# Experts: one gather and one addition of 4 KB rows each, empty slots left out, matmuls held to program order

## The chip, the cores and the metric

The kernel runs on one core of a Trainium2 chip. The metric is the device time of one execution in microseconds (us). The engines of the core are TensorE (PE, with its weight load PEld), VectorE (DVE), ScalarE (ACT), GpSimd (POOL) and SyncE (SP); 16 DMA engines move data between HBM and SBUF. SP, ACT and POOL issue the DMAs.

## What is computed

The reference is a transformer block with a mixture of experts, followed by a second block (FFN, attention, state space, FFN, gated embedding). Only the experts of the first block matter here. Every one of 1024 tokens of 1024 features chooses two of 32 experts; an expert is a SwiGLU of width 256. Everything is float32.

```python
weights = g_p * e_p / jnp.sum(e_p, axis=-1, keepdims=True)      # two per token
expert = g_sel * EXPERTS_PER_GROUP + e_idx
...
def block_ffn(args):
    xb_i, e = args
    return (jax.nn.silu(xb_i @ w_gate[e]) * (xb_i @ w_up[e])) @ w_down[e]
...
out = jnp.zeros((T + 1, D), yb.dtype).at[buf_tok].add(yb * buf_w[:, None])
...
x = layer_norm(DEEPNORM_ALPHA * x + (1.0 + gt2) * y, ln2_g[l], ln2_b[l])
```

## The kernel before, in words

**Ahead of the experts.** `wo_last` (L1091) makes, for each of 8 groups of 128 tokens, the input of the experts (`h2`) and the residual already scaled (`x1`), and stores both in DRAM: `h2d` and `r1d`, each as two tensors of [1024, 512], one for each half of the features (L1088, L1111, L1114). The router (L1116 and the lines up to L1353) counts the tokens of each expert and builds, with 16 small matmuls, one column per expert with the tokens in its 104 slots (`CAP`). `slot_rows` (L1314) makes two tables of it: `table`, in which an empty slot names row 0, and `dest`, in which an empty slot names a row beyond 1023.

**One expert.** `gather` (L1355) fetches the rows of its slots with two indirect DMAs from GpSimd, one for each half of 512 features (2 KB a row), into tiles of the pool D. `expert_rows` (L1365) transposes them on TensorE, eight transposes, and splits the result into a high and a low part. `expert_up` (L1377) multiplies them with the gate and the up weights, 16 contraction steps of three matmuls (`mm3`: high x high, high x low, low x high), and forms silu(gate) x up, called the product here. `expert_turn` (L1389) transposes the product, two transposes, into `aT`. `expert_down` (L1398) multiplies it with the down weights, four matmuls of 512 columns, scales each half into a tile `y` of the small pool tmp, and adds it to `r1d` in DRAM with an indirect DMA that accumulates, one for each half; rows beyond 1023 are left out there. A tile may be written again only when those who read it are done, so `y`, the product `a` and other users of tmp wait for each other.

**Weights.** An expert has 3 x 1 MB of weights. `load_weights` (L1139) loads each matrix with four DMAs of 256 KB on SP's queue, in program order. Gate and up weights go to pool A (26 tiles), are split into high and low parts (`split_weights`, L1151; every fourth low part is made on GpSimd, the others on VectorE), and their parts lie in B and W. Down weights are used unsplit; `wide` (L1131) places them in turn in buffers of the pools raw, sub and tmpG.

**The loop** (L1414) runs over 32 experts. In turn e it gathers the rows of e + 2, splits the gate weights of e + 1, issues up of e, the row transposes of e + 1, down of e - 1 and the transposes of the product of e, splits the up weights of e + 1, and issues the loads of gate and up of e + 4 and of down of e + 2. A scheduler with a model of its own then sets the order on each engine; only what `keep_in_program_order` marks keeps its place among the marked. Here that is SP's weight loads; `pin` (L1363) is the identity, so the matmuls of the experts may move.

**Behind the loop** stands a second loop for experts with more than 104 tokens (L1444), which with these inputs runs no turn: the trace has 64 gathers, two for each expert. Then the first FFN begins with loads of `r1d`.

Of the kernel before, what the change touches and what calls it, by code (L numbers as in the profile page):

```python
# [32 lines left out]
T = 1024  # L33
# [184 lines left out]
def kernel(ctx: ExitStack, tc: tile.TileContext, I, C, out, taps=None, stop=99):  # L218
# [869 lines left out]
    h2d = [dr.tile([T, NH], F32, name=f"h2d{n}") for n in range(2)]  # L1088
    r1d = [dr.tile([T, NH], F32, name=f"r1d{n}") for n in range(2)]
    bl = bkB("bl")  # L1090
    def wo_last(t):  # L1091
# [14 lines left out]
        for n in range(2):  # L1106
            x = tD("x1")
            nc.scalar.activation(x, xr[:, half(n)], AF.Identity, bias=nm, scale=rs)
            nc.vector.tensor_mul(h2[n], x, sc2[n])
            nc.vector.tensor_add(h2[n], h2[n], sh2[n])  # L1110
            nc.sync.dma_start(h2d[n][t * 128:(t + 1) * 128, :], h2[n])  # L1111
            nc.gpsimd.tensor_mul(x, x, lg[n])
            nc.gpsimd.tensor_add(x, x, lb[n])
            nc.sync.dma_start(r1d[n][t * 128:(t + 1) * 128, :], x)  # L1114
            tap("x1", lambda a: a[t * 128:(t + 1) * 128, half(n)], x)
# [15 lines left out]
    def wide(n):  # L1131

        o = []
        for al in ((raw, raw), (raw, sub), (sub, None))[n]:
            t_ = al("wr") if al else None
            o += [t_[:, half(i)] if al else tmpG("wr") for i in range(2)]
        return o

    def load_weights(e, part, n=1, up=None):  # L1139
# [57 lines left out]
    def expert_loads(e, part=("gate", "up", "down")):  # L1197
        if e < 32:
            loaded[e] = loaded.get(e, []) + load_weights(e, part, e % 3)
# [14 lines left out]
    expert_loads(2)  # L1214
    expert_loads(3, ("gate", "up"))
    if stop <= 3:
        return

# [95 lines left out]
    def slot_rows(ps, n, src, dst):  # L1314
# [8 lines left out]
    table, dest, wslot = ctile("table", 32, I32), ctile("dest", 32, I32), const(32, "wslot")  # L1323
    tabled = slot_rows(bt[0:CAP, 0:32], 32, table, dest)
# [29 lines left out]

    def gather(rows):  # L1355

        xg = [tD("xg") for _ in range(2)]
        for n in range(2):
            nc.gpsimd.indirect_dma_start(out=xg[n][0:CAP, :], out_offset=None, in_=h2d[n],
                                         in_offset=bass.IndirectOffsetOnAxis(ap=rows[0:CAP, :], axis=0))  # L1360
        return xg

    pin = lambda i: i  # L1363

    def expert_rows(xg):  # L1365

        xT = []
        for h in range(2):
            b = bkB()
            for k in range(4):  # L1370
                nc.tensor.transpose(b[:, k * CAP:(k + 1) * CAP], xg[h][0:CAP, k * 128:(k + 1) * 128], ident[0:CAP, 0:CAP])
# [17 lines left out]
    def expert_turn(a_):  # L1389
        b = bkB()  # L1390
        for f in range(2):
            nc.tensor.transpose(b[:, f * CAP:(f + 1) * CAP], a_[:, f * 128:(f + 1) * 128], ident[0:CAP, 0:CAP])
        aT = tD("aT")[:, 0:2 * CAP]
# [14 lines left out]
    gathered[0] = gather(table[:, 0:1])  # L1408
    gathered[1] = gather(table[:, 1:2])
# [4 lines left out]
    for e in range(32):  # L1414
        if e < 30:
            gathered[e + 2] = gather(table[:, e + 2:e + 3])
# [27 lines left out]
    with tc.For_i(0, nc.values_load(nextra[0:1, 0:1], min_val=0, max_val=XMAX)) as ik:  # L1444
# [13 lines left out]
        xrows, xdest, xws = small(1, "xrows", I32), small(1, "xdest", I32), small(1, "xws")  # L1458
        slot_rows(bt[0:CAP, 0:1], 1, xrows, xdest)
# [7 lines left out]
        expert_down(expert_turn(expert_up(expert_rows(gather(xrows)), ws)), wd, xdest, xws)  # L1467
# [23 lines left out]
    def second_loads():  # L1491
        for t in range(8):
            for n in range(2):
                xr2[t, n] = tA("xr2")
                tc.keep_in_program_order(nc.sync.dma_start(xr2[t, n], r1d[n][t * 128:(t + 1) * 128, :]))
# [1218 lines left out]
```

## Time and profile before

| | us |
|---|---|
| median of 3 runs (3518.17 to 3523.24) | 3522.32 |
| the profiled execution | 3528.53 |
| its span, first to last instruction | 3526.7 |
| TensorE busy | 3286.4 (93%) |
| VectorE busy | 2444.1 (69%) |
| GpSimd busy | 1598.0 (45%) |
| ScalarE busy | 1484.4 (42%) |

A profile is one execution. Its times count from the start of the span; the experts run from 770 to 1175 us. TensorE's "granted clock" is the share of its full speed (2.4 GHz) that it was given. The "DMA share" is the mean busy share of the 16 DMA engines; it can exceed 1 a little, since transfers overlap. In the queue rows q1 is SP's queue and q0 GpSimd's.

### The profile page before, as it was taken

The numbers are of one execution on the slowest core, as the hardware profiler recorded it, in microseconds if no ns is written. First come the engines' busy times: TensorE is split into PE (matmuls) and PEld (weight loads), VectorE is DVE, ScalarE is ACT, GpSimd is POOL, SyncE is SP. The second block draws the span as 40 slices with busy tenths as digits, with TensorE's granted clock in tenths as the row PEclk, the third lists the DMA queues.
The fourth block names the chain that finished last, engine by engine and source line by source line (L and its number), as shares of the span: only waits on it lengthen the run. The fifth ranks groups of instructions, "written<-read, shape, count | busy, mean of one in ns | idle before, by whom it ended". The sixth has DMA issues, their size and how long they took to land. (4 is left out here: it accounts for less than half of the span.)

```text
span 3526.7 us, 49670 instructions
## 1 busy us (share of the span) xinstructions
PE 3286.4 (93%) x16788; PEld 2678.4 (76%) x16788; DVE 2444.1 (69%) x4146; ACT 1484.4 (42%) x2818; POOL 1598.0 (45%) x1228
## 2 busy tenths in 40 slices
PE   7998998979889789999999899999999999998998
PEld 5687887767666568887788777778778788886888
DVE  8857467777666676665976885577655866668685
ACT  5554434235554543232443233455623433324456
POOL 3533002357667467778511435522001587776011
PEclk9998999979999899999999999989999999999999
DMA  8421114579999523326643363543145223347433
GB/s 291 147 72 41 34 43 132 181 253 284 318 308 293 162 86 112 99 96 226 216 138 102 123 203 120 148 135 97 51 142 201 78 97 119 99 177 245 125 99 114
DMA packets 305650, 529.33 MB, mean 150 GB/s; under 512 B 67889, under 2 KB 82610, under 8 KB 305394
## 3 DMA queue, kind: packets, MB, share of 16 engines
q1 hardware_dynamic: 265328, 449.64, 39.4%
q10 hardware_dynamic: 25570, 53.91, 4.9%
q0 software_dynamic: 14496, 22.59, 2.8%
q8 instruction: 134, 2.20, 0.3%
q14 instruction: 122, 1.00, 0.1%
HBM read 409.55 MB, written 121.62 MB: 151 GB/s over the span
## 5 line engine op out<-in xcount | busy, mean ns | idle before, releaser
L284 PE MATMUL b<-x,wh 128*128 128x512 f32 x992 | 392.2, 396 | 3.9 <-ACT wh L277 3.9
L288 PE MATMUL b<-x,wl 128*128 128x512 f32 x992 | 390.4, 394 | 1.8 <-DVE wl L278 1.7
L287 PE MATMUL b<-x,wh 128*128 128x512 f32 x992 | 388.5, 392 | 0.0
L343 POOL TENSOR_TENSOR acc<-acc,sqt 128x512 f32<-128x512 f32 x42 | 62.7, 1492 | 519.1 <-ACT sqt L342 515.6
L278 DVE TENSOR_TENSOR wl<-S,wh 128x512 fp32r<-128x512 f32 x176 | 209.2, 1192 | 84.6 <-ACT wh L277 49.9
L284 PE MATMUL b<-ah,wh 128*128 128x512 f32 x560 | 221.0, 397 | 9.8 <-ACT wh L277 9.8
L288 PE MATMUL b<-ah,wl 128*128 128x512 f32 x560 | 213.9, 395 | 14.6 <-DVE wl L278 14.5
L288 PEld LDWEIGHTS b<-x,wl 128*128 128x128 f32 x992 | 186.7, 188 | 47.8 <-DVE wl L278 3.5
L287 PE MATMUL b<-al,wh 128*128 128x512 f32 x560 | 222.3, 397 | 0.0
L284 PEld LDWEIGHTS b<-x,wh 128*128 128x128 f32 x992 | 187.1, 189 | 45.2 <-ACT wh L277 4.9
L1158 DVE TENSOR_TENSOR wl<-wr,wh 128x512 fp32r<-128x512 f32 x186 | 168.4, 919 | 74.3 <-ACT wh L1157 69.6
L287 PEld LDWEIGHTS b<-x,wh 128*128 128x128 f32 x992 | 186.9, 188 | 42.7
L277 ACT CAST wh<-S 128x512 fp32r<-128x512 f32 x176 | 108.3, 618 | 242.5 <-PE b L287 203.2
L278 DVE TENSOR_TENSOR wl<-raw,wh 128x512 fp32r<-128x512 f32 (+1 forms) x187 | 144.7, 781 | 78.7 <-ACT wh L277 74.2
L1157 ACT CAST wh<-wr 128x512 fp32r<-128x512 f32 x256 | 157.0, 620 | 83.4 <-PE b L287 41.5
L277 ACT CAST wh<-raw 128x512 fp32r<-128x512 f32 (+1 forms) x187 | 112.2, 610 | 178.3 <-PE b L287 88.4
L288 PE MATMUL b<-hnh,wl 128*128 128x512 f32 (+1 forms) x480 | 178.4, 372 | 0.0
L284 PE MATMUL b<-hnh,wh 128*128 128x512 f32 (+1 forms) x480 | 178.3, 372 | 0.0
L287 PE MATMUL b<-hnl,wh 128*128 128x512 f32 (+1 forms) x480 | 177.1, 369 | 0.0
L1749 POOL TENSOR_TENSOR c<-c,rb 128x512 f32<-128x512 f32 x80 | 124.3, 1563 | 108.4 <-DVE c L1745 108.4
L284 PE MATMUL b<-wh,xTh 128*104 128x256 f32 x512 | 154.5, 302 | 4.2 <-ACT xTh L277 4.2
L284 PE MATMUL b<-xh,wh 128*128 128x512 f32 x384 | 151.4, 400 | 4.2 <-ACT xh L1528 2.4
(890 smaller groups left out, 9768.9 us busy)
## 6 DMA issues: line engine op xcount, KB each, us to landing
ffn_pair<-c SPq DMA_DIRECT2D x140, 256.0 KB
act<-ffn_pair SPq DMA_DIRECT2D x140, 256.0 KB
wr<-in_moe_w_gate SPq DMA_DIRECT2D x128, 256.0 KB
wr<-in_moe_w_up SPq DMA_DIRECT2D x128, 256.0 KB
wr<-in_moe_w_down SPq DMA_DIRECT2D x128, 256.0 KB
wm<-in_w_mod SPq DMA_DIRECT2D x96, 256.0 KB
wu<-in_ffn_u SPq DMA_DIRECT2D x40, 512.0 KB
wg<-in_ffn_g SPq DMA_DIRECT2D x80, 256.0 KB
```

The source lines that it names most:

```text
L277: nc.scalar.copy(hi, src)
L278: return nc.vector.tensor_sub(lo, src, hi.bitcast(F32)).ins
L284: i = nc.tensor.matmul(ps, wh, xh, start=s, stop=False)
L287: nc.tensor.matmul(ps, wh, xl, start=False, stop=False)
L288: nc.tensor.matmul(ps, wl, xh, start=False, stop=e)
L343: eng.tensor_add(acc, acc, t)
L1157: nc.scalar.copy(hi[i], w[i])
L1158: (eng or (nc.gpsimd if i == 3 else nc.vector)).tensor_sub(lo[i], w[i], hi[i].bitcast(F32))
L1749: nc.gpsimd.tensor_mul(o, o, rb[h])
```

## The change

`h2d` and `r1d` become one tensor of [1024, 1024] each. An expert's rows are fetched by one gather and added by one DMA, of 4 KB rows. The gather takes `dest`, leaves rows beyond 1023 out, and fills one of two fixed tiles (pool sub), which are zeroed once; `table` is gone. Down weights move to pool D (10 tiles), `y` to raw, `aT` to tmpG. Down of e + 1 is loaded ahead of gate and up of e + 4, where down of e + 2 was loaded behind them. `pin` becomes `keep_in_program_order`, for the transposes, the down matmuls and the first matmul of each `mm3` in `expert_up`.

```diff
-    h2d = [dr.tile([T, NH], F32, name=f"h2d{n}") for n in range(2)]
-    r1d = [dr.tile([T, NH], F32, name=f"r1d{n}") for n in range(2)]
+    h2d = dr.tile([T, 1024], F32, name="h2d")
+    r1d = dr.tile([T, 1024], F32, name="r1d")
...
-            w = wide(n) if name == "down" else [tA("wr") for _ in range(4)]
+            w = [(tD if name == "down" else tA)("wr") for _ in range(4)]
...
-    expert_loads(2)
-    expert_loads(3, ("gate", "up"))
+    for e in range(2, 4):
+        expert_loads(e, ("gate", "up"))
...
+    slots = [sub("xg") for _ in range(2)]
+    for xg in slots:
+        nc.gpsimd.memset(xg[0:CAP, :], 0.0)
...
-        i = V.tensor_scalar(src[r], ps, -1.0, 0.0, op0=ALU.add, op1=ALU.max)
         V.tensor_scalar(f[r], ps, 0.5, beyond[r], op0=ALU.is_lt, op1=ALU.mult)
-        V.scalar_tensor_tensor(dst[r], ps, -1.0, f[r], op0=ALU.add, op1=ALU.add)
-        return i.ins
+        return V.scalar_tensor_tensor(rows[r], ps, -1.0, f[r], op0=ALU.add, op1=ALU.add).ins
...
-        xg = [tD("xg") for _ in range(2)]
-        for n in range(2):
-            nc.gpsimd.indirect_dma_start(out=xg[n][0:CAP, :], out_offset=None, in_=h2d[n],
-                                         in_offset=bass.IndirectOffsetOnAxis(ap=rows[0:CAP, :], axis=0))
+        xg = next(turns)
+        nc.gpsimd.indirect_dma_start(out=xg[0:CAP, :], out_offset=None, in_=h2d,
+                                     in_offset=bass.IndirectOffsetOnAxis(ap=rows[0:CAP, :], axis=0),
+                                     bounds_check=T - 1, oob_is_err=False)
         return xg
 
-    pin = lambda i: i
+    pin = tc.keep_in_program_order
...
-                mm3(b[0:CAP, i * 256:(i + 1) * 256], xT[k // 4][0][:, c], xT[k // 4][1][:, c], *w(k * 256, 256), k == 0, k == 7)
+                mm3(b[0:CAP, i * 256:(i + 1) * 256], xT[k // 4][0][:, c], xT[k // 4][1][:, c], *w(k * 256, 256), k == 0, k == 7, True)
...
-        aT = tD("aT")[:, 0:2 * CAP]
+        aT = tmpG("aT")[:, 0:2 * CAP]
...
+        y = raw("y")
         for n in range(2):
             b = bkP()[0:CAP]
             for f in range(2):
-                nc.tensor.matmul(b, aT[:, f * CAP:(f + 1) * CAP], wd[2 * f + n], start=f == 0, stop=f == 1)
-            y = tmp("y")[0:CAP]
-            V.scalar_tensor_tensor(y, b, ws[0:CAP], gt2[n][0:CAP], op0=ALU.mult, op1=ALU.mult)
-            nc.gpsimd.indirect_dma_start(out=r1d[n], out_offset=bass.IndirectOffsetOnAxis(ap=dst[0:CAP, :], axis=0), in_=y,
-                                         in_offset=None, bounds_check=T - 1, oob_is_err=False, compute_op=ALU.add)
+                pin(nc.tensor.matmul(b, aT[:, f * CAP:(f + 1) * CAP], wd[2 * f + n], start=f == 0, stop=f == 1))
+            V.scalar_tensor_tensor(y[0:CAP, half(n)], b, ws[0:CAP], gt2[n][0:CAP], op0=ALU.mult, op1=ALU.mult)
+        nc.gpsimd.indirect_dma_start(out=r1d, out_offset=bass.IndirectOffsetOnAxis(ap=dst[0:CAP, :], axis=0), in_=y[0:CAP, :],
+                                     in_offset=None, bounds_check=T - 1, oob_is_err=False, compute_op=ALU.add)
...
+        if e:
+            expert_loads(e + 1, ("down",))
         expert_loads(e + 4, ("gate", "up"))
-        if e:
-            expert_loads(e + 2, ("down",))
```

On TensorE, between two experts in the later part of the loop (here expert 23), the order before was the following. L288 with `xTl` is the last matmul of up, L1392 transposes the product `a`, L1371 the next expert's rows, L1402 is down of the expert before, and L284 the first matmul of the next up.

```order
L288 MATMUL b<-wh,xTl 104x256
L1392 MATMUL b<-sqc,a 128x104 x2
L1371 MATMUL b<-sqc,xg 128x104 x8
L1402 MATMUL b<-wr,aT 104x512 x4
L284 MATMUL b<-wh,xTh 104x256
```

In the change the same place reads as follows, for every expert from 1 to 30 (L1367 is the transposes of rows, L1399 down, L1388 the transposes of the product).

```order
L288 MATMUL b<-wh,xTl 104x256
L1367 MATMUL b<-sqc,xg 128x104 x8
L1399 MATMUL b<-wr,aT 104x512 x4
L1388 MATMUL b<-sqc,a 128x104 x2
L284 MATMUL b<-wh,xTh 104x256
```

The transposes of the product have moved behind down; before, their place changed from expert to expert.

On SP the loads of the third expert's down weights stood behind its up weights (`wr_7294` is the last of these) and ahead of the fourth expert's gate.

```order
L1146 DMA wr_7293<-in_moe_w_up 128x512
L1146 DMA wr_7294<-in_moe_w_up 128x512
L1146 DMA wr_7299<-in_moe_w_down 128x512 x2
L1146 DMA wr_7300<-in_moe_w_down 128x512
L1146 DMA wr_7301<-in_moe_w_down 128x512
L1146 DMA wr_7306<-in_moe_w_gate 128x512
```

In the change they stand behind the fifth expert's up weights (`wr_7728` is the last) and behind the load of a register (`nextra`, the number of overflow turns), ahead of the sixth expert's gate.

```order
L1138 DMA wr_7728<-in_moe_w_up 128x512
L1440 TENSOR_LOAD nextra_7554
L1440 ISA x2
L1138 DMA wr_7855<-in_moe_w_down 128x512
L1138 DMA wr_7856<-in_moe_w_down 128x512
L1138 DMA wr_7857<-in_moe_w_down 128x512
L1138 DMA wr_7858<-in_moe_w_down 128x512
L1138 DMA wr_7863<-in_moe_w_gate 128x512
```

From there on SP's order is the same in both: down of one expert, then gate and up of the one three further on.

On GpSimd an expert's DMAs and its two low parts of weights (`wl`) stood as follows in the middle of the loop; `xg` is a gather, `r1d` an addition, 0 and 1 are the halves.

```order
L1405 DMA r1d0_6487<-y_8877,dest_7538 1024x512
L1359 DMA xg_9083<-h2d0_6485,table_7537 104x512
L1359 DMA xg_9084<-h2d1_6486,table_7537 104x512
L1158 TENSOR_TENSOR wl_9249<-wr_8914,wh_9248 128x512
L1158 TENSOR_TENSOR wl_9207<-wr_8773,wh_9206 128x512
L1405 DMA r1d1_6488<-y_8885,dest_7538 1024x512
```

In the change there is one gather, into one of the two tiles in turn, and one addition.

```order
L1354 DMA xg_7318<-h2d_6485,dest_7536 104x1024
L1401 DMA r1d_6486<-y_8698,dest_7536 1024x1024
L1150 TENSOR_TENSOR wl_9063<-wr_8742,wh_9062 128x512
L1150 TENSOR_TENSOR wl_9020<-wr_8604,wh_9019 128x512
L1354 DMA xg_7317<-h2d_6485,dest_7536 104x1024
L1401 DMA r1d_6486<-y_8844,dest_7536 1024x1024
```

All additions now go to one tensor, `r1d`, where they went to two.

## Rows read from the trace of the kernel before

**Rows 1.** The page: span, and busy time of each engine.

```profile
span 3526.7 us, 49670 instructions
PE 3286.4 (93%) x16788; PEld 2678.4 (76%) x16788; DVE 2444.1 (69%) x4146; ACT 1484.4 (42%) x2818; POOL 1598.0 (45%) x1228
```

**Rows 2.** Busy time by stretch: PE, PEld, DVE, ACT, POOL, clock, DMA share, GB/s.

```profile
783.00:800.00 17.00, 16.09 (x113) 13.63 (x112) 13.73 (x19) 13.00 (x23) 8.02 (x6) 0.96 0.48 152
...
800.00:1130.00 330.00, 298.72 (x1846) 227.10 (x1845) 225.17 (x304) 178.03 (x334) 229.96 (x163) 0.96 1.02 307
```

**Rows 3.** Waits of SP, 800 to 1130 us: us in total, times, longest.

```profile
SPq L1146 <- DMA wr<-in_moe_w_down: 68.5, 89, 2.3
SPq L1146 <- DMA wr<-in_moe_w_up: 67.5, 92, 2.1
SPq L1146 <- DMA wr<-in_moe_w_gate: 56.4, 95, 2.0
SPq L1146 <- DVE wl L1158: 6.0, 20, 0.7
```

**Rows 4.** Timeline of TensorE: start, duration; up of experts 4, 8, 10, 31, down.

```profile
820.60 0.68 PE L284 MATMUL b<-wh,xTh 128*104 128x256 f32 x1
...
837.51 3.60 PE L1402 MATMUL b<-wr,aT 128*104 128x512 f32 x8
...
860.50 0.68 PE L284 MATMUL b<-wh,xTh 128*104 128x256 f32 x1
...
885.21 0.36 PE L284 MATMUL b<-wh,xTh 128*104 128x256 f32 x1 [1.52 <-ACT xTh L277]
...
1146.82 0.68 PE L284 MATMUL b<-wh,xTh 128*104 128x256 f32 x1
...
1157.23 3.68 PE L1402 MATMUL b<-wr,aT 128*104 128x512 f32 x8 [0.42 <-ACT aT L1394]
```

**Rows 5.** Waits of TensorE, 800 to 1165 us: us in total, times, longest.

```profile
PE b L1392 <- DVE a L1386: 14.5, 8, 2.8
PE b L1371 <- DMA xg<-h2d,table: 7.1, 4, 2.4
```

**Rows 6.** A stretch at low clock, columns as in rows 2.

```profile
887.00:893.00 6.00, 5.46 (x26) 5.46 (x27) 3.81 (x6) 2.51 (x5) 2.58 (x3) 0.50 0.99 312
```

**Rows 7.** GpSimd's groups, first 800 to 1130, then 770 to 1160 us.

```profile
L1405 POOL DMA_INDIRECT r1d<-y,dest x54 | 95.6, 1771 | 28.6 <-DVE y L1404 12.0 <-issue 6.9 <-DMA r1d<-y,dest 2.9
...
L1359 POOL DMA_INDIRECT xg<-h2d,table x54 | 61.4, 1138 | 15.6 <-issue 13.5 <-PE b L288 0.9 <-DMA r1d<-y,dest 0.6
...
L1359 POOL DMA_INDIRECT xg<-h2d,table x64 | 72.1, 1127 | 18.4 <-issue 15.3 <-PE b L288 0.9 <-DMA r1d<-y,dest 0.6
```

**Rows 8.** DMA queues, 800 to 1130 us: packets, MB, share of 16 engines.

```profile
q1 hardware_dynamic: 45399, 82.68, 77.8%
q0 software_dynamic: 11952, 18.20, 23.8%
```

**Rows 9.** The same, 765 to 799 us, ahead of the first addition.

```profile
q0 software_dynamic: 800, 2.23, 19.5%
```

**Rows 10.** The same, 762 to 768 us, weights alone.

```profile
q1 hardware_dynamic: 1261, 2.30, 103.6%
```

**Rows 11.** Timeline of SP's queue: start, duration of the issues.

```profile
756.95 2.94 SPq L1146 DMA_DIRECT2D wr<-in_moe_w_down  x4
...
783.25 4.63 SPq L1146 DMA_DIRECT2D wr<-in_moe_w_gate  x4
...
1117.52 5.36 SPq L1146 DMA_DIRECT2D wr<-in_moe_w_up  x4
```

**Rows 12.** The tensor r1d: who waited for it (us, times), and landing times.

```profile
  ACT a L1385: 12.0, 4
...
  POOL r1d L1405: 5.2, 5
...
DMA to landing us min/median/max: 4.6/8.0/10.1
```

More of the change, by code (lines that the diff above doesn't have):

```diff
@@ L1110, in wo_last @@
             nc.vector.tensor_add(h2[n], h2[n], sh2[n])
-            nc.sync.dma_start(h2d[n][t * 128:(t + 1) * 128, :], h2[n])
+            nc.sync.dma_start(h2d[t * 128:(t + 1) * 128, half(n)], h2[n])
             nc.gpsimd.tensor_mul(x, x, lg[n])
             nc.gpsimd.tensor_add(x, x, lb[n])
-            nc.sync.dma_start(r1d[n][t * 128:(t + 1) * 128, :], x)
+            nc.sync.dma_start(r1d[t * 128:(t + 1) * 128, half(n)], x)
             tap("x1", lambda a: a[t * 128:(t + 1) * 128, half(n)], x)
@@ L1129, in router, with load_weights @@
         return i.ins
[L1131 to L1139, printed above, removed]
+    def load_weights(e, part, up=None):
         ws = []
@@ L1198, in expert_loads @@
         if e < 32:
-            loaded[e] = loaded.get(e, []) + load_weights(e, part, e % 3)
+            loaded[e] = loaded.get(e, []) + load_weights(e, part)
     last = None
@@ L1312, with slot_rows @@
     ple_steps(4, placed)
-    def slot_rows(ps, n, src, dst):
+    def slot_rows(ps, n, rows):
         f = small(n, f"sr{n}")
         r = slice(0, CAP)
-        i = V.tensor_scalar(src[r], ps, -1.0, 0.0, op0=ALU.add, op1=ALU.max)
         V.tensor_scalar(f[r], ps, 0.5, beyond[r], op0=ALU.is_lt, op1=ALU.mult)
-        V.scalar_tensor_tensor(dst[r], ps, -1.0, f[r], op0=ALU.add, op1=ALU.add)
-        return i.ins
-    table, dest, wslot = ctile("table", 32, I32), ctile("dest", 32, I32), const(32, "wslot")
-    tabled = slot_rows(bt[0:CAP, 0:32], 32, table, dest)
+        return V.scalar_tensor_tensor(rows[r], ps, -1.0, f[r], op0=ALU.add, op1=ALU.add).ins
+    dest, wslot = ctile("dest", 32, I32), const(32, "wslot")
+    tabled = slot_rows(bt[0:CAP, 0:32], 32, dest)
     V.tensor_copy(wslot[0:CAP], bt[0:CAP, 32:64])
@@ L1353 @@
     XMAX = (2 * T - 2) // CAP
+    turns = itertools.cycle(slots)
     def gather(rows):
[L1357 to L1360 removed]
+        xg = next(turns)
+        nc.gpsimd.indirect_dma_start(out=xg[0:CAP, :], out_offset=None, in_=h2d,
+                                     in_offset=bass.IndirectOffsetOnAxis(ap=rows[0:CAP, :], axis=0),
+                                     bounds_check=T - 1, oob_is_err=False)
         return xg
[L1363 removed]
+    pin = tc.keep_in_program_order
     def expert_rows(xg):
@@ L1401, in expert_down @@
             for f in range(2):
-                nc.tensor.matmul(b, aT[:, f * CAP:(f + 1) * CAP], wd[2 * f + n], start=f == 0, stop=f == 1)
-            y = tmp("y")[0:CAP]
-            V.scalar_tensor_tensor(y, b, ws[0:CAP], gt2[n][0:CAP], op0=ALU.mult, op1=ALU.mult)
-            nc.gpsimd.indirect_dma_start(out=r1d[n], out_offset=bass.IndirectOffsetOnAxis(ap=dst[0:CAP, :], axis=0), in_=y,
-                                         in_offset=None, bounds_check=T - 1, oob_is_err=False, compute_op=ALU.add)
-    gathered[0] = gather(table[:, 0:1])
-    gathered[1] = gather(table[:, 1:2])
+                pin(nc.tensor.matmul(b, aT[:, f * CAP:(f + 1) * CAP], wd[2 * f + n], start=f == 0, stop=f == 1))
+            V.scalar_tensor_tensor(y[0:CAP, half(n)], b, ws[0:CAP], gt2[n][0:CAP], op0=ALU.mult, op1=ALU.mult)
+        nc.gpsimd.indirect_dma_start(out=r1d, out_offset=bass.IndirectOffsetOnAxis(ap=dst[0:CAP, :], axis=0), in_=y[0:CAP, :],
+                                     in_offset=None, bounds_check=T - 1, oob_is_err=False, compute_op=ALU.add)
+    gathered[0] = gather(dest[:, 0:1])
+    gathered[1] = gather(dest[:, 1:2])
     gt2 = brow(modrows, 3, tE, nc.gpsimd)
@@ L1415 @@
         if e < 30:
-            gathered[e + 2] = gather(table[:, e + 2:e + 3])
+            gathered[e + 2] = gather(dest[:, e + 2:e + 3])
         if 0 < e < 31:
@@ L1457 @@
                 nc.tensor.matmul(bt[0:CAP, 0:2], R[:, 0:CAP], R[:, 128:130], start=t + a == 0, stop=t + a == 8)
-        xrows, xdest, xws = small(1, "xrows", I32), small(1, "xdest", I32), small(1, "xws")
-        slot_rows(bt[0:CAP, 0:1], 1, xrows, xdest)
+        xdest, xws = small(1, "xdest", I32), small(1, "xws")
+        slot_rows(bt[0:CAP, 0:1], 1, xdest)
         V.tensor_copy(xws[0:CAP], bt[0:CAP, 1:2])
@@ L1466 @@
         ws = split_weights(ws)
-        expert_down(expert_turn(expert_up(expert_rows(gather(xrows)), ws)), wd, xdest, xws)
+        expert_down(expert_turn(expert_up(expert_rows(gather(xdest)), ws)), wd, xdest, xws)
     def rms(srcs):
@@ L1494, in second_loads @@
                 xr2[t, n] = tA("xr2")
-                tc.keep_in_program_order(nc.sync.dma_start(xr2[t, n], r1d[n][t * 128:(t + 1) * 128, :]))
+                tc.keep_in_program_order(nc.sync.dma_start(xr2[t, n], r1d[t * 128:(t + 1) * 128, half(n)]))
     class Seven:
```

4 lines of the change are left out of this document (2 added, 2 removed).

## The prediction

> **What bounds the kernel now.** I read the page first. TensorE is busy 93% of 3526.7 us [rows 1], so in most stages it sets the time. But every changed line, the two DRAM tensors apart, belongs to the experts, so I cut their stretch out and read it by itself. From 800 to 1130 us the 16 DMA engines are busy 1.02 of the time at 307 GB/s, while TensorE has 298.7 of 330 us, at a granted clock of 0.96 [rows 2]. Who feeds the DMA engines? SP waits for the landing of its own earlier weight loads for 68.5 + 67.5 + 56.4 = 192 of the 330 us; for a buffer that VectorE has yet to free it waits 6.0 us [rows 3]. A queue that nearly always waits for its own transfers is limited by them. So here the end is set by **bytes on the DMA engines**, with TensorE close behind: while its weights were loaded ahead it does an expert in (860.50 - 820.60) / 4 = 10.0 us, later in (1146.82 - 885.21) / 21 = 12.5 us [rows 4].
>
> What TensorE waits for in that stretch [rows 5]: the product that is to be transposed, 14.5 us in 8 waits, then gathered rows (7.1 us). After idle time it also runs slower: from 887 to 893 us the granted clock is 0.50, the 1.2 GHz level [rows 6]. These are losses of the order on TensorE. As long as weights arrive at 12.5 us per expert they cost little; they matter at the end, where TensorE trails the last weights.
>
> **The change part by part.** The sum is made against the profiled execution, 3528.5 us (span 3526.7, [rows 1]); the runs' median, 3522.3, lies 6.2 us lower, and the difference is carried over to it.
>
> *Gathers.* There are 54 in the stretch, 54 additions and 104 slots a gather [rows 7]; a gather of 104 rows of 2 KB is 0.213 MB, so they move 11.5 MB. GpSimd's queue (q0) has 18.2 MB and 23.8% of 330 us = 78.5 us of all engines [rows 8]; 6.7 MB of that are the additions. Of 32 x 104 = 3328 slots only 1024 x 2 = 2048 are filled, for each token has two experts and no expert overflows (64 gathers, none from the overflow loop, [rows 7]). Leaving empty slots out saves 38.5% of the bytes, 4.4 MB. Price of a gathered MB: low, from a stretch with gathers and no additions, 19.5% of 34 us for 2.23 MB = 3.0 us per MB [rows 9]; high, all of q0 alike, 78.5 / 18.2 = 4.3 us. So 13 to 19 us; I take 16, the middle, since the low row lies where the weights ran undisturbed. Nothing, if an empty slot still costs its row.
>
> *Relief of the weights.* Alone they need 103.6% of 6 us for 2.30 MB = 2.7 us per MB [rows 10], beside q0 77.8% of 330 us for 82.7 MB = 3.1 us [rows 8]. All of that excess would be 33 us. q0 shrinks by 16 of 78.5, a fifth, so at most 6.6 us come back; I take 4.
>
> *Additions.* The same bytes in half as many, 4 KB rows. No row shows a 4 KB addition. By bytes 0; if the price were per row, half of what is left of q0, (78.5 - 11.5 x 3.0) / 2 = 22 us. I take 0: weights and gathers, with rows of 2 KB in DRAM both, cost 2.7 and 3.0 us per MB, close to each other, so bytes are the nearer rule. The Trainium skill (page "DMA: Bandwidth & Descriptors", section "Why small descriptors are slow (HBM only)") has a fixed overhead of some 3 cycles a packet, which between 2 and 4 KB would be an estimated 2%, under 2 us here; it speaks against the 22, and no run here shows it.
>
> *Loads that come later.* The third expert's down weights used to sit in other buffers and were loaded at 757 us; now they stand behind the register load on SP, in the ten D buffers, two of which come free only when the first expert's down matmuls are over. The next expert's eight gate and up loads, issued from 783 us on, stand behind them [rows 11]. The DMA engines were busy 0.48 of the time from 783 to 800 us [rows 2], so this room is lost: two of the four down loads and those eight, ten of 256 KB, 2.62 MB at 3.1 us = 8 us later. From there the order on SP is the old one. The first expert's product is now transposed before the second expert starts, with no down matmuls ahead of it: one wait like those for the product, 14.5 / 8 = 2 us [rows 5], bounds 0 and 4; it holds back the first down as well, and so the loads.
>
> So the last gate and up weights come 16 + 4 - 8 - 2 = **10 us earlier**. They are issued by 1122.9 us [rows 11]; with eight loads in flight (2.1 MB at 307 GB/s) they have landed at about 1130, an estimate.
>
> *TensorE in program order.* Now every expert reads: up, transposes of the next rows, down of the one before, transposes of the product. Between up and the last stand eight transposes and 3.6 us of down matmuls [rows 4], more than the longest wait for the product, 2.8 us [rows 5]; and the product no longer shares its buffers with y, on whose addition ScalarE's activation waited 12.0 us [rows 12]. The 14.5 us go. While DMA bounds, that is worth nothing by itself: what is late next is the down weights of expert e+2, which lie behind gate and up of e+4 in SP's queue. At the end it is worth the lag. Before, the last down matmul starts at 1157.2, 27 us behind the estimated 1130 [rows 4]. The path that remains: four down loads (1.05 MB at 307 GB/s) 3.4, one round from down to down 10.0, the next down 3.6 [rows 4], the last transposes and their copy some 1 = 18 us; I add 2 for one spell at low clock: **7 us less**. Bounds: 0, and 9.
>
> *GpSimd.* It issues 32 gathers and 32 additions fewer, 1.13 and 1.77 us each [rows 7], about 90 us; it is not waited for by weights that DMA brings late, so 0 on the path. Its two added memsets stand well before the stretch, beside normalisation work of other engines: 0; 1 us if they are not covered.
>
> *Tail.* After the last down matmul two additions are issued one behind the other, 1.77 us each [rows 7], and everything waits for the second to land. One remains, of twice the size: **2 us less** (0 to 2). The FFN behind it is untouched; its rows are still read in 2 KB halves.
>
> Sum: 10 + 7 + 2 = 19, rounded to **20 us less: 3508.5 in a profile, 3502 as a median.** What a measurement of this kernel can tell from no change is 0.2%, 7 us.
>
> **The rivals.**
>
> *A: the change saves no bytes* (an empty slot costs as much as a row). For it: nothing before shows a gather with a bound. Against: the addition has one, and its queue carries 18.2 MB, which leaves 6.7 for it, not the 11.5 of all slots [rows 8]. Then the weights come 10 us later, the end gains 9: about 0, **3521**.
>
> *B: slower, one chain of additions.* Before, the halves went to two tensors, each with its own chain; now each addition must wait for the one before it to land, and it does so on GpSimd's queue, ahead of the next gather and of the low parts of the weights. An addition takes 4.6 to 10.1 us to land, 8.0 in the median [rows 12]; an expert must take no less than that. It decides from about 12 us. With rows twice as long the landing could go, between 8 and 16, to 13.5: 27 experts x (13.5 - 12.5) = 27 us later, less the 9 at the end: **+18, 3540**. Against: only 5.2 us of waits for it before [rows 12], and the part of a landing that grows with bytes is small (64 rows over 16 engines). The Trainium skill ("DMA: Bandwidth & Descriptors", section "Rules for kernel authors") says that an addition beside another to the same bytes must wait for the earlier one's semaphore; by that rule the chain can't be cut, and the trace has the wait.
>
> *C: more than bytes.* If additions are priced per row (22 us) the DMA engines stop bounding, and TensorE's 10.0 us per expert does. Then 10 + 22 + 7 + 2: **about 40 less, 3482**. The floor is 23 x 10.0 us behind the 860.5 of expert 8: up of the last at 1090 in place of 1147, 56 less.
>
> **How the numbers follow.** The forecast has 0.55; its own bounds (gathers 13 to 19, relief 0 to 6.6, late loads and start 8 to 12, end 0 to 9, tail 0 to 2) run from 1 less to 29 less, 3493 to 3521. A 0.18, B 0.11, C 0.16. The range 3484 to 3523 takes in the forecast, A and half of C; it leaves out B and C's far half, 0.19. Faster by over 7 us: 0.50 of the forecast, C's 0.16 and 0.05 of A: 0.71. Within 7 us: 0.16. Slower: B and the rest of A, 0.13.
>
> **What would show it.** Right: q0 moves about 2048 x 4 KB of gathers where it moved 13.6 MB; the DMA engines still stand near 1.0 from 800 us to the last load; an expert takes about 11.5 us late in the stage; last gate and up issued near 1113; no wait of the product's transposes over 1 us but the first; the last down matmul starts 15 to 20 us earlier. Wrong: q0's bytes unchanged (A); GpSimd waiting for additions over 20 us, weights' low parts late (B); DMA engines clearly under 0.9 with TensorE at 10 us an expert (C); or gathers, now only two ahead, that TensorE waits for.

## The result, and the profile after

The changed kernel takes **3548.75 us** (median of 5 runs, 3545.82 to 3554.64); the kernel before, run beside it, 3522.32. The ratio is 1.0069, 95% interval 1.0053 to 1.0085. The forecast was 3502, the range 3484 to 3523: the change is slower where it was forecast faster.

First the page of the kernel after (compare rows 1), then its stretches (columns as in rows 2). The first two stretches run from the last product of the embeddings, the mark at which the experts begin: 24.7 us from there, and on to the last gate load. The same two stretches of the kernel before stand ahead of them.

```profile
span 3544.0 us, 49530 instructions
PE 3286.2 (93%) x16788; PEld 2684.7 (76%) x16788; DVE 2438.4 (69%) x4145; ACT 1478.2 (42%) x2818; POOL 1543.0 (44%) x1166
```

```profile
774.06:798.80 24.74, 19.34 (x130) 17.02 (x129) 17.33 (x38) 15.22 (x27) 11.44 (x10) 0.86 0.69 228
...
774.06:1113.69 339.63, 303.56 (x1877) 232.49 (x1876) 231.39 (x327) 184.13 (x344) 229.56 (x166) 0.95 0.99 301
```

```profile
767.97:792.71 24.74, 20.09 (x130) 17.81 (x129) 17.15 (x37) 15.39 (x28) 9.42 (x8) 0.86 0.43 136
...
767.97:1107.98 340.01, 298.56 (x1859) 231.35 (x1858) 221.18 (x323) 176.21 (x342) 177.75 (x109) 0.95 0.93 286
...
800.00:1130.00 330.00, 290.60 (x1792) 223.15 (x1791) 211.07 (x298) 167.89 (x328) 179.65 (x107) 0.95 0.97 297
...
1160.00:1184.00 24.00, 0.16 (x1) 0.16 (x1) 2.58 (x4) 4.24 (x8) 5.10 (x4) 0.52 0.56 131
```

Busy times of TensorE hardly differ; the time went into gaps. In this profile the experts begin 6.1 us earlier than in that of the kernel before, so stretches of the same clock time do not hold the same work. In the 24.7 us behind the mark the DMA engines stand at 0.43 where they were at 0.69; up to the last gate load both kernels take the same time (339.6 and 340.0 us), with the engines busy 0.99 of it before and 0.93 after; and from 1160 to 1184 us TensorE does next to nothing. The queues from 800 to 1130 us (compare [rows 8]), the issues on SP's queue ([rows 11]) and TensorE at the end ([rows 4]):

```profile
q1 hardware_dynamic: 46306, 84.31, 78.1%
q0 software_dynamic: 7540, 13.29, 18.1%
```

```profile
777.43 15.19 SPq L1138 DMA_DIRECT2D wr<-in_moe_w_down  x4
792.71 2.04 SPq L1138 DMA_DIRECT2D wr<-in_moe_w_gate  x4
...
1107.98 2.64 SPq L1138 DMA_DIRECT2D wr<-in_moe_w_gate  x4
```

```profile
1153.56 3.68 PE L1399 MATMUL b<-wr,aT 128*104 128x512 f32 x8 [0.48 <-ACT aT L1390]
...
1183.84 0.80 PE L284 MATMUL b<-ph 128*128 128x512 f32 x1 [26.60 <-DMA xr<-r1d]
```

The experts can be cut into five pieces by marks that all kernels of this study have, read from the timelines (starts of instructions): the last product of the embeddings ahead of the experts (before 774.06, after 767.97); **start**, from it to the gate load of the sixth expert (before 783.25, after 792.71); **pace**, on to the gate load of the last expert (1113.69; 1107.98); **trail**, on to the down matmuls of the last expert (1157.23; 1153.56); **additions**, on to the issue of the last addition (1167.12; 1172.28); **restart**, on to TensorE's next product (1174.96; 1183.84). All in us; "again" is a second profile of the same kernel. The pieces come from one execution each, which lies up to 13 us from the median beside it (e2 13.0 above, e7c 10.7 below).

| kernel | median | start | pace | trail | additions | restart | sum |
|---|---|---|---|---|---|---|---|
| before | 3522.3 | 9.2 | 330.4 | 43.5 | 9.9 | 7.8 | 400.9 |
| before, again | | 11.0 | 330.2 | 41.0 | 9.9 | 7.6 | 399.8 |
| after | 3548.8 | 24.7 | 315.3 | 45.6 | 18.7 | 11.6 | 415.9 |
| after, again | | 24.7 | 318.5 | 45.2 | 19.9 | 11.4 | 419.8 |
| e1 two chains | 3532.1 | 24.7 | 311.9 | 43.2 | 15.0 | 12.8 | 407.6 |
| e3 additions first | 3531.2 | 23.9 | 317.3 | 38.4 | 7.5 | 11.7 | 398.8 |
| e4 all slots | 3559.5 | 24.7 | 329.2 | 47.2 | 17.5 | 12.0 | 430.5 |
| e5 before, skipping | 3520.6 | 11.1 | 318.2 | 49.0 | 11.2 | 7.4 | 396.8 |
| e2 no pin | 3547.5 | 21.0 | 315.1 | 48.2 | 24.4 | 13.6 | 422.3 |
| e6 loads swapped | 3534.6 | 7.0 | 326.8 | 46.6 | 11.8 | 11.7 | 403.9 |
| e7 first + swapped | 3531.1 | 5.7 | 323.4 | 50.9 | 7.5 | 12.1 | 399.7 |
| e7c gather free | 3527.6 | 6.6 | 321.6 | 44.8 | 7.6 | 11.6 | 392.1 |
| e10 7c, two chains | 3524.7 | 6.4 | 323.9 | 42.6 | 7.5 | 13.9 | 394.2 |
| e11 before, skip + pin | 3522.1 | 11.2 | 324.6 | 40.3 | 11.2 | 7.8 | 395.1 |
| e12 e11, additions first | 3566.1 | 11.5 | 335.8 | 66.0 | 10.3 | 7.7 | 431.4 |
| e13 before, pin | 3519.2 | 9.7 | 327.5 | 42.8 | 9.8 | 7.3 | 397.1 |
| e14 one load swapped | 3535.7 | 6.1 | 336.0 | 40.8 | 7.5 | 11.4 | 401.7 |

In the first profiles the experts lose 15.5 at the start, win 15.1 in the pace, and lose 2.1 + 8.8 + 3.8 at the end: 15 us. The second profiles make it 20.0. Start and pace are best read together: in the kernel before the DMA engines had room just behind the gate load that parts them (0.48 from 783 to 800 us, [rows 2]), in the changed one ahead of it, so part of what the start loses comes back as pace. Together they are 339.6 before and 340.0 after, in the second profiles 341.2 and 343.3. The kernel before beside the later groups of runs had medians of 3520.8 to 3523.3. (Expectations quoted below measure a "stage" to a product 7 to 8 us behind the restart: 408.7 us before and 423.3 after are 400.9 and 415.9 in this table.)

The end on GpSimd's queue, first the additions behind the start of the last down matmuls in the kernel before (1157.23), then kernel after:

```profile
1158.52 1.60 POOL L1405 DMA_INDIRECT r1d<-y,dest  x1 [0.92 <-issue]
1165.22 1.60 POOL L1405 DMA_INDIRECT r1d<-y,dest  x1 [5.10 <-DVEq L1444]
1167.12 1.60 POOL L1405 DMA_INDIRECT r1d<-y,dest  x1 [0.30 <-issue]
```

```profile
1150.86 1.60 POOL L1401 DMA_INDIRECT r1d<-y,dest  x1 [6.74 <-DVE a L1382]
1157.82 1.60 POOL L1401 DMA_INDIRECT r1d<-y,dest  x1 [5.36 <-DMA r1d<-y,dest]
1164.76 1.59 POOL L1401 DMA_INDIRECT r1d<-y,dest  x1 [5.34 <-DMA r1d<-y,dest]
1172.28 1.59 POOL L1401 DMA_INDIRECT r1d<-y,dest  x1 [5.92 <-DMA r1d<-y,dest]
```

The last expert's down matmuls start at 1153.56, and then three more additions have to be issued, each only when the one before it has landed: some 7 us a round. The tensor `r1d` (who waited for it, and landing times; compare [rows 12]), and TensorE's waits from 800 to 1184 us (compare [rows 5]):

```profile
  DVE y L1400: 34.0, 8
  POOL r1d L1401: 33.6, 8
...
DMA to landing us min/median/max: 6.0/9.5/14.1
```

```profile
PE b L284 <- DMA xr<-r1d: 26.6, 1, 26.6
PE b L1388 <- DVE xTl L278: 21.4, 11, 3.1
PE b L1399 <- DVE y L1400: 17.2, 7, 4.8
```

GpSimd waits 33.6 us for landings (5.2 before), VectorE 34.0 for a buffer of `y` whose addition has not landed (9.7 before).

### The profile page after: what moved, and what is told of

It is laid out like the page before. It is cut to its first block, busy times and chain, and to the rows that moved or that the text cites. A ratio compares the mean times of both kernels' runs of the same rounds, so it can differ in the third digit from the quotient of the medians.

```text
span 3544.0 us, 49530 instructions
## 1 busy us (share of the span) xinstructions
PE 3286.2 (93%) x16788; PEld 2684.7 (76%) x16788; DVE 2438.4 (69%) x4145; ACT 1478.2 (42%) x2818; POOL 1543.0 (44%) x1166
## 5 line engine op out<-in xcount | busy, mean ns | idle before, releaser
L284 PE MATMUL b<-x,wh 128*128 128x512 f32 x992 | 392.1, 397 | 3.9 <-ACT wh L277 3.9
L288 PE MATMUL b<-x,wl 128*128 128x512 f32 x992 | 390.4, 394 | 0.8 <-DVE wl L278 0.8
L288 PE MATMUL b<-ah,wl 128*128 128x512 f32 x560 | 215.2, 398 | 16.6 <-DVE wl L278 16.6
L284 PE MATMUL b<-ah,wh 128*128 128x512 f32 x560 | 221.0, 398 | 8.8 <-ACT wh L277 8.8
L284 PEld LDWEIGHTS b<-x,wh 128*128 128x128 f32 x992 | 187.0, 189 | 46.0 <-ACT wh L277 4.9
L288 PEld LDWEIGHTS b<-x,wl 128*128 128x128 f32 x992 | 186.6, 188 | 46.0 <-DVE wl L278 1.6
L284 PE MATMUL b<-hnh,wh 128*128 128x512 f32 (+1 forms) x480 | 177.3, 370 | 0.1
L288 PE MATMUL b<-hnh,wl 128*128 128x512 f32 (+1 forms) x480 | 177.0, 369 | 0.0
L284 PE MATMUL b<-xh,wh 128*128 128x512 f32 x384 | 152.6, 403 | 5.7 <-ACT xh L1524 4.5
L278 DVE TENSOR_TENSOR al<-act,ah 128x512 fp32r<-128x512 f32 x140 | 133.5, 959 | 30.0 <-ACT ah L277 30.0
```

Of the source, the lines that this page charges most:

```text
L278: return nc.vector.tensor_sub(lo, src, hi.bitcast(F32)).ins
L284: i = nc.tensor.matmul(ps, wh, xh, start=s, stop=False)
L288: nc.tensor.matmul(ps, wl, xh, start=False, stop=e)
```

## The experiments

Three theories. **L**: additions are issued late and one behind the other; they hold `y` back during the stage and are drained at its end. **S**: the loads start late and so give back what the gathers save. **E**: the order held on TensorE is itself the cost.

Eight of the runs' medians are of 11 or 12 executions, the others of 4 to 7; the two repeated profiles have one.

**e1, two chains.** The residual is two tensors again:

```diff
-    r1d = dr.tile([T, 1024], F32, name="r1d")
+    r1d = [dr.tile([T, NH], F32, name=f"r1d{n}") for n in range(2)]
...
-        nc.gpsimd.indirect_dma_start(out=r1d, out_offset=bass.IndirectOffsetOnAxis(ap=dst[0:CAP, :], axis=0), in_=y[0:CAP, :],
+            nc.gpsimd.indirect_dma_start(out=r1d[n], out_offset=bass.IndirectOffsetOnAxis(ap=dst[0:CAP, :], axis=0), in_=y[0:CAP, half(n)],
```

> The changed kernel, but the residual in DRAM is two tensors again and an expert's rows are added in two halves of 2 KB rows, each half with a chain of its own. Gathers, y in one tile of raw and the order on TensorE stay as changed. Theory L (additions one behind the other and late): at the end two additions are in flight at once, so the 26.6 us in which TensorE waits for the last rows shrink to about 16; TensorE's waits for y shrink; about 3530 us, 3522 to 3540. Rival P (the price per byte of a 4 KB addition): the mean q0 packet per MB falls clearly below the changed kernel's and the time too. Rival E (the order on TensorE or the later loads): nothing moves, 3543 to 3555.

Measured 3532.07, ratio to before 1.0022 (1.0008 to 1.0035): some 17 us less than after. Of the sum 8.3 us go, in pace, trail and additions; the rest of the 17 is not in the experts of this profile. The time is as expected, the signs only in part: GpSimd's waits for landings fall from 33.6 to 14.4 us, but the gap of TensorE at the end only from 26.6 to 24.2, and its waits for `y` do not shrink (17.2 after):

```profile
PE b L284 <- ACT ph L1171: 24.2, 1, 24.2
PE b L1399 <- DVE y L1400: 22.5, 7, 6.1
```

The price was read too. q0 from 800 to 1130 us:

```profile
q0 software_dynamic: 11353, 13.48, 19.4%
```

That is 19.4% of 330 us for 13.48 MB, 4.75 us per MB, against 18.1% and 13.29 MB, 4.49, with 4 KB rows. So additions of 4 KB rows are not dearer, as rival P wanted, but a little cheaper: 0.26 x 13.3 = 3.5 us (by the second profile of the changed kernel, 17.8% for 12.98 MB or 4.53, it is 3 us).

**e3, additions first.** The instruction's `ins` is returned by `expert_down` as `sent`:

```diff
-        if e < 30:
-            gathered[e + 2] = gather(dest[:, e + 2:e + 3])
-        if 0 < e < 31:
-            early[e + 1] = split_weights(loaded[e + 1][:1])
+        with tc.issue_after(sent) if sent else ExitStack():
+            if e < 30:
+                gathered[e + 2] = gather(dest[:, e + 2:e + 3])
+            if 0 < e < 31:
+                early[e + 1] = split_weights(loaded[e + 1][:1])
```

> The changed kernel, with the gather of expert e + 2 and the split of gate of e + 1 queued on GpSimd behind the addition of the expert before, so that an addition no longer stands behind the weight parts of later experts; one chain of 4 KB additions stays. Theory L: at most two additions are left when the last gather is issued, where there were five; TensorE's wait for the last rows falls from 26.6 to about 14 us, VectorE's waits for the buffers of y from 34 to under 10; 12 to 25 us less than the changed kernel, 3524 to 3537. Rival B of the prediction in its pure form (a landing is longer than an expert): no gain, GpSimd waits for landings over 100 us. Rival E (order on TensorE, later loads): 3543 to 3555.

Measured 3531.19, 1.0026 (1.0009 to 1.0043), 17.6 us less than after; the sum falls by 17.1, of which 11.2 in the additions and 7.2 in the trail. Same DMAs, same rows, same single chain: what the edit sets is their place on GpSimd's queue. (With it the scheduler's order on VectorE and ScalarE changed too: weight splits now stand between the splits of the rows.) The end of GpSimd's queue, and who waited for `r1d`:

```profile
1130.64 1.62 POOL L1401 DMA_INDIRECT r1d<-y,dest  x1 [4.61 <-DMA wr<-in_moe_w_down]
...
1138.13 1.61 POOL L1401 DMA_INDIRECT r1d<-y,dest  x1 [3.35 <-DVE y L1400]
1147.39 1.60 POOL L1401 DMA_INDIRECT r1d<-y,dest  x1 [7.65 <-DVE y L1400]
1154.51 1.59 POOL L1401 DMA_INDIRECT r1d<-y,dest  x1 [5.52 <-DMA r1d<-y,dest]
```

```profile
  POOL r1d L1401: 5.5, 1
...
DMA to landing us min/median/max: 5.4/8.9/10.2
```

Additions now wait for `y`, as they should, and only the last for a landing. (Four, not two, still follow the last gather; in the changed kernel there were seven, not the five of the expectation. Only two follow the start of the last down matmuls at 1146.96, where it was three.) In all five variants of the changed kernel that hold the gate split behind the addition (e3, e7, e7c, e10, e14) the additions take 7.5 or 7.6 us, in the changed kernel 18.7: L is shown for this part. How much of the trail's 7.2 us is owed to the order on the other engines is not shown. A landing takes 8.9 us, less than an expert, so the chain alone does not set the pace (rival B in its pure form falls). The place has a price: the gather stands behind the addition, and TensorE waits 20.4 us in 14 places for rows.

**e4, all slots.** The gathers take a list with row 0 in empty slots again:

```diff
-            gathered[e + 2] = gather(dest[:, e + 2:e + 3])
+            gathered[e + 2] = gather(table[:, e + 2:e + 3])
```

> The changed kernel, but its gathers take a list without empty slots left out (they fetch row 0), as before: 38% more rows gathered, 5.2 MB over the 32 experts. If bytes on the DMA engines set the end: 19 us slower than the changed kernel, 3564 to 3572. Theory L (the stage waits for additions, the DMA engines have room): 0 to 8 us slower, 3546 to 3557.

Measured 3559.45, 1.0100 (1.0074 to 1.0125): 10.7 us more than after, the pace 13.9 longer than in its first profile and 10.7 than in its second. Between the two expectations: the saved bytes are real, and of the 19 us that they were expected to be worth 10.7 are on the path. Start is the same 24.7 us in both, so this is the cleanest price of the bytes here.

**e5, before with skipping alone.**

```diff
-        xg = [tD("xg") for _ in range(2)]
+        xg = next(turns)
...
-                                         in_offset=bass.IndirectOffsetOnAxis(ap=rows[0:CAP, :], axis=0))
+                                         in_offset=bass.IndirectOffsetOnAxis(ap=rows[0:CAP, :], axis=0),
+                                         bounds_check=T - 1, oob_is_err=False)
```

> The kernel before, with one part of the change alone: its two gathers of 2 KB rows take the list dest and leave empty slots out, into four fixed tiles of pool D. If bytes on the DMA engines set the end there, as the prediction says, and 19 us of the 16 engines go (the gathers' packets of the changed kernel against before): 3500 to 3512. If the order on TensorE or the additions set it, within 6 us of 3522.

Measured 3520.58, ratio 0.9995 (0.9978 to 1.0012): no change. The pace is 12.2 us shorter, but the trail 5.5 longer, additions 1.3 and start 1.9; of 12 us some 4 are left. Weights that arrive sooner find TensorE behind: it waits for the product 22.5 us in 14 places, where it was 14.5 in 8 [rows 5].

```profile
PE b L1397 <- DVE a L1391: 22.5, 14, 3.4
```

**e2, no pin.** `pin = lambda i: i`, and the first matmul of `mm3` in `expert_up` free.

> The changed kernel without its last part: the experts' matmuls and transposes are not held to program order on TensorE, the scheduler sets their order as before. Theory L and S (additions one behind the other and late; loads that start late): the order on TensorE is worth little, 3543 to 3555, as the changed kernel. If the order held is itself a cost, 3525 to 3540; if it is a gain hidden behind the others, 3556 to 3565.

Measured 3547.49, 1.0070 (1.0056 to 1.0084): as the changed kernel. The order held is not the cost (E falls). Nor did it take the wait for the product away: without it there is no such wait either. TensorE's two longest waits from 770 to 1195 us, but for that at the end:

```profile
PE b L284 <- ACT xTh L277: 21.5, 16, 3.6
PE b L1399 <- DVE y L1400: 9.1, 9, 4.1
```

**e13** holds the order in the kernel before, and changes nothing else:

> The kernel before with one part of the change alone: the experts' TensorE work held to program order; all slots gathered. If bytes on the DMA engines set the stage, only the end can gain: 0 to 7 us, stage 402 to 409, 3515 to 3523. If the waits for the product were on the path (14.5 us in 8 of them): 3507 to 3513. If holding the order costs: over 3526.

Measured 3519.16, 0.9997 (0.9985 to 1.0010). The sum is some 3 us smaller, the time the same. With the order held the wait for the product is still there (17.9 us, [rows 5] had 14.5), and one for `xTl` beside it:

```profile
PE b L1392 <- DVE xTl L278: 18.7, 8, 5.7
PE b L1392 <- DVE a L1386: 17.9, 7, 5.6
```

**e6, loads swapped.**

```diff
-        if e:
-            expert_loads(e + 1, ("down",))
         expert_loads(e + 4, ("gate", "up"))
+        if e:
+            expert_loads(e + 1, ("down",))
```

> The changed kernel with one swap on SyncE's queue: an expert's turn queues gate and up of e + 4 first and down of e + 1 behind them, so that the gate weights of the sixth expert no longer stand behind down of the third, which waits for a buffer. In the changed kernel that gate load was issued 24.7 us after the last products of the embeddings began, before it was 9.1 us. Theory S (this late start takes back what the gathers save): issued at 10 to 15 us, last gate load 10 to 15 us earlier, the time 8 to 15 us less than the changed kernel, unless the additions at the end take it: 3534 to 3545. Rival (the loads are late only because TensorE's or VectorE's buffers come late, whatever the order): 3545 to 3555.

Measured 3534.64, 1.0039 (1.0021 to 1.0057), 14 us less than after. The gate load comes 17.7 us sooner after the mark, more than expected, but the pace is 11.5 longer, so that the last gate load gains only 6 us: down weights now arrive late, and TensorE waits for them. Another 6.9 us are gained in the additions, of which two and not three follow the last down matmuls here, and TensorE's waits for `y` fall from 17.2 to 2.0 us; so the 14 us are not S alone.

```profile
774.73 4.39 SPq L1138 DMA_DIRECT2D wr<-in_moe_w_gate  x4
```

```profile
PE b L1399 <- DMA wr<-in_moe_w_down: 25.3, 15, 7.1
```

**e7 and e7c** join e3 and e6; in e7c only the gate split, not the gather, is queued behind the addition.

> The swap of the loads and, besides, the additions queued on GpSimd ahead of the next gather and gate split (as in the run with additions first). If both causes are real and lie one behind the other, they add up: 17 us of the one and 8 to 15 of the other less than the changed kernel, 3516 to 3526, at or under the kernel before. If they hide each other, about 3531, as the additions first alone.

> As the run before (swap, additions ahead of the gate split), but the gather is left free to go ahead of the addition. In the run with additions first TensorE waited 20.4 us in 14 places for gathered rows; these waits should go. If they were on the path, 5 to 15 us less than with the gather behind the addition, 3505 to 3518; if the weights set the end, the same within 4 us.

Measured 3531.11 (1.0030, 1.0016 to 1.0044) and 3527.62 (1.0012, 0.9999 to 1.0025). The two causes do not add up in e7; with the gather free the sum is the smallest of all, 392.1, and the time 21 us under the changed kernel, but not under the one before. **e10** gives it two chains:

> The swapped loads, the additions ahead of the gate split, the gather left free, and the residual in two tensors again, so that an expert's rows are added in two halves of 2 KB in two chains. Against the same with one chain of 4 KB (stage 399.0 us, time 3527.6): if an addition's landing still delays something there, 4 to 10 us less in the stage and about 3520; if the queue order alone did it, the stage stays within 4 us of 399 and the time within 5 of 3528.

Measured 3524.71 (1.0016, 1.0000 to 1.0031), the sum within 2.1 of e7c: once additions stand in the right place, a second chain is worth nothing that these runs can tell.

**e11** is the kernel before with skipping and the order held; **e12** also queues the gate split behind both additions.

> The kernel before with two parts of the change: empty slots left out of the gathers (2 KB rows, as in the run with that alone: stage 403.5 us, 3520.6) and the experts' TensorE work held to program order. Buffers of the down weights, order of the loads, y and the two chains stay as before. The forecast's term for the order (7 us at the end, 8 waits for the product gone): stage 393 to 400, 3508 to 3516. If the order is worth nothing: 403 and 3517 to 3524.

> As the run before (kernel before, empty slots left out, TensorE in program order), with the gate split of each expert queued on GpSimd behind the additions of the one before. Theory L: the last additions are issued 3 to 6 us sooner after the last down matmul, 3 to 6 us less than without; if the two chains of 2 KB rows never held anything there, the same within 3 us.

Measured 3522.07 (1.0000, 0.9988 to 1.0012) and 3566.07 (1.0123, 1.0100 to 1.0146). e11 comes out as if the order were worth nothing: the wait for the product goes down from e5's 22.5 us to 10.3, but one for `xTl` (15.2) takes its place. e12 is a miss on the other side: the weight parts on GpSimd stand behind two additions for each expert, and TensorE waits for them:

```profile
PE b L287 <- POOL wl L1158: 48.6, 19, 3.9
```

So "additions first" is no rule: on the changed kernel it helped, on this one it cost 44 us. That two additions stand ahead is not enough to explain it: e10 has two as well, one behind the other ahead of the same split, and TensorE's wait for these parts is 1.9 us there.

```profile
PE b L287 <- POOL wl L1150: 1.9, 3, 0.9
```

What else differs (two gathers of 2 KB rows for each expert, the buffers of `y`, the order of the loads) was not taken apart.

**e14** swaps the loads in the second turn alone, on top of e7c's queue order.

> As the run with the gather left free (additions ahead of the gate split), but the loads are swapped only in the second turn: gate and up of the sixth expert go ahead of down of the third, which waits for a buffer; from the third turn on the order is that of the changed kernel again. Theory S: the gate load of the sixth expert is issued at 6 to 10 us as with all swapped, TensorE's 25 to 28 us of waits for down weights fall under 10, and the stage comes to 388 to 396 us, 3510 to 3520. If something else sets the stage (TensorE at 10 to 12 us an expert with its waits), 397 to 404 and 3522 to 3530.

Measured 3535.66 (1.0035, 1.0021 to 1.0049). A miss: the start is short (6.1 us) and the waits for down weights are gone, but the pace is 336.0, and TensorE now waits for VectorE:

```profile
PE b L1388 <- DVE xTl L278: 38.9, 13, 6.3
```

**The two kernels, profiled again.**

> The kernel before, profiled a second time. If stage lengths are stable, the experts take 408.7 us within 4 and no low-clock spell is added in the stage behind 2347 us (51 us from there to the third quarter of its products, in the first profile 92.3). If they are draws, 10 us or more apart.

> The changed kernel, profiled a second time. If the 9 us in the late stage belong to the kernel, they are there again (103.1 against 92.3 us in that stretch) and the experts take 423.3 within 4. If they are a draw, they are gone and the whole difference lies in the experts.

The experts' sums repeat within 1.1 and 3.9 us. A late stage does not: between the same two products it took, in the kernel before (first), after (second) and after again (third; columns as in rows 2)

```profile
2382.30:2439.20 56.90, 52.85 (x396) 46.14 (x394) 42.85 (x129) 32.38 (x83) 14.75 (x20) 0.92 0.40 116
```

```profile
2391.40:2457.50 66.10, 61.82 (x396) 54.26 (x394) 43.49 (x127) 32.50 (x83) 15.52 (x20) 0.78 0.35 101
```

```profile
2396.80:2452.60 55.80, 51.74 (x398) 45.41 (x394) 44.09 (x132) 32.37 (x83) 15.07 (x20) 0.94 0.43 127
```

In the first profile of the changed kernel the clock stands at the 1.2 GHz level (0.50) from 2417.5 to 2434 us, a little behind an idle of TensorE:

```profile
2414.92 0.34 PE L2422 MATMUL ye<-cr,xim 64*128 64x128 f32 x1 [1.18 <-POOL bt L2467]
```

```profile
2417.50:2434.00 16.50, 16.50 (x66) 14.48 (x66) 2.36 (x17) 6.93 (x18) 0.00 (x0) 0.50 0.35 99
```

In the second that idle is not there, and the clock is 1.00 in the same stretch. The 9 us, at a mean clock of 0.78, are a draw of one execution; the stage's work is the same. Seven of the seventeen profiles show 56 to 57 us in that stretch, one 61 and nine 66 to 68: of the six of kernels built on the one before two are long (e11, e12), of the eleven of the changed kernel and its variants seven. Whether the change makes the long form more frequent is not shown.

## Why the prediction was wrong

**Right, the bytes on the DMA engines.** The gathers were to save 16 us of the engines and the weights 4. With skipping alone (e5) q0 falls from 23.8% to 19.0% of 330 us, which is 16 us; in the changed kernel from 18.20 to 13.29 MB and to 18.1%. Weights go from 77.8% for 82.68 MB to 78.1% for 84.31, 3.11 to 3.06 us per MB, or 4 us; the second profiles, 3.08 and 3.08, do not repeat that. The additions' price goes mostly by bytes (3.5 us in e1's comparison, not rival C's 22). The Trainium skill (page "DMA: Bandwidth & Descriptors", section "Why small descriptors are slow (HBM only)") has a fixed overhead for each packet, by which an estimate of under 2 us was made; the 3.5 measured is more, but of that order.

**Too high, what they are worth on the path: 20, measured 11 to 14.** That is what the pace loses with all slots back (e4); with skipping alone (e5) the last gate load comes 10 to 12 us earlier behind the mark. The step took the engines to stay at 1.02 of the time; they fall to 0.97 in the changed kernel, so other waits share the stage then. The sign "last gate and up issued near 1113" came by luck: they were issued from 1108 us on because the experts began 6.1 us earlier in that profile.

**Right in its wait, loads that come later: 8 + 2.** By the issue of the sixth expert's gate load they come 13.7 to 15.5 us later; but part of that returns as pace (see the table). In the same 24.7 us behind the mark the DMA engines are busy 0.69 before and 0.43 after, in the second profiles 0.73 and 0.43: 6.4 to 7.4 us of them are lost. The swap that takes the wait away brings the last gate load 6 us forward alone (e6) and 12 us from e3 to e7, where the order on GpSimd is the same. The step named one of the two waits of SP from 765 to 800 us, that for the first expert's down matmuls; it did not have the other, for the store of an embeddings' product (`py`), which lies in pool D as well:

```profile
SPq L1138 <- DMA ple_d<-py: 11.0, 2, 7.5
SPq L1138 <- PE b L1399: 10.1, 2, 9.7
```

**Wrong above all, the tail and GpSimd: 2 less and 0, measured 8.8 + 3.8 more.** The step "after the last down matmul two additions are issued; one remains" took an addition to follow its down matmul. On GpSimd's queue it does not. Before, three halves were still to be issued when the last down matmuls started, and two chains ran side by side: 9.9 us. Now it is three whole additions at 7 us a round, in one chain: 18.7. (The Trainium skill, page "DMA: Bandwidth & Descriptors", section "Rules for kernel authors", says that an accumulating DMA must wait for an earlier one to the same bytes. By that rule the chain can't be cut, and the trace agrees: rounds of 7 us.) And "not waited for by weights" set GpSimd to 0, though it holds the additions and they hold `y`. e3 shows both: with the additions ahead on GpSimd's queue 11.2 us go in that piece, and the waits of `y` for landings are gone; the time falls by 17.6. Rival B had the place (one chain, ahead of other work on GpSimd, wait over 20 us) but the wrong deciding point: a landing needn't outlast an expert, it is enough that the additions stand late in the queue when the weights have ended. The restart's 3.8 us are in all kernels built on the changed one, with two chains as well (12.8, 13.9); they were not taken apart.

**Wrong, TensorE in program order: 7 less, measured 2.1 to 4.2 more in the trail.** The wait for the product did go, but not by the order: it is gone without it too (e2) and stays with it in the kernel before (e13). What took it away is not shown; that the product no longer shares its buffers with `y` fits, and no run has that alone. Two others came, seen above: 21.4 us for `xTl` and 17.2 for `y`. The transposes of the product need a PSUM bank of the pool bB, which has two, and both hold the next expert's transposed rows until VectorE has split them; VectorE has weight splits queued ahead of that. The step asked only whether the product would be ready, not whether its output had room. With the order held in the kernel before (e13) the same wait is there, 18.7 us in 8.

Together: 10 less to the last gate load became 0.4 more, and 9 less at the end 14.7 more: 15 us more, where 19 less were summed. The second profiles give 2.0 and 18.0, 20 us. The medians differ by 26.4; of the rest, the late stage at low clock gives 9 in executions that have it. How often timed runs have it is **open**, for they have no trace.

Open too: why the sum does not fall under 392 in any variant. The saved bytes show in the pace of e5, but what follows takes most of them back, and each mend moved TensorE's waits: to gathered rows (e3), down weights (e6, e7c), the split of the rows (e14), GpSimd's weight parts (e12). The edits also shift the scheduler's order on VectorE and ScalarE, which no run held fixed. No version was found that is clearly faster than the kernel before: e13 and e5 cannot be told from it.

## What to carry to other kernels

Where several queues share a stage near their limits, saved bytes are worth what the start and the end leave of them: count when the first load can be issued after a buffer change, and what still stands on each queue when the last load lands. Two half transfers in two chains may be slower in bytes and quicker at the end than one whole transfer in one chain; count the items left times a round. And where the order of matmuls is changed, ask of an output bank, not only of an input, who frees it.

## What was not expected of the hardware

In one chain of additions a round took 7 us (1157.82 to 1164.76) although the issue takes 1.6 and the DMA engines stand at 0.56. And executions of one program differ by a whole low-clock stretch: the late stage took 66.1 us at a mean clock of 0.78 or 55.8 at 0.94, which is more than most of the effects measured here. One profile is not enough to place 10 us in a kernel of 3.5 ms.
